# A decoder layer with sparse attention on one core: attention blocks from small to large, feature tiles and the output projection as work between them, the spatial gate per token tile

## The chip, the cores and the metric

One Trainium2 chip, of which one core runs the kernel. The metric is the device time of one execution in microseconds (us), the median of several runs. The engines of the core are TensorE (PE in the profile; PEld is its loading of weights), VectorE (DVE), ScalarE (ACT), GpSimd (POOL) and SyncE (SP), which issues most of the DMAs. Each engine works through its instructions in one fixed order and waits by semaphores for the others.

## The reference, cut to what matters

One inference step of a one-layer hybrid decoder: 1024 prompt tokens and eight sample sequences of one token each, model width 1024, all in fp32. In this cut, `u, v, z_a` belong to a gated MLP of eight channel groups of 64, the rest to a sparse attention of eight query heads and two key heads.

```python
hn = rms_norm(x, norm_g)
u, v, z_a, q, kc, vc, ks, vs, kw, vw, g, z_b = split(hn @ w_in)
vn = layer_norm(v, ln_g, ln_b)
s = einsum('bnsgc,gts->bntgc', vn, w_s * tril) + b_s     # per chunk of 128 tokens
a_out = u * s * silu(z_a)
kcc, vcc = compress(kc, w_ck, pe_ck), compress(vc, w_cv, pe_cv)   # 32 tokens -> 1, stride 16
for each block of 128 queries:
    o = gate0 * attention(q, kcc, vcc) + gate1 * attention(q, selected ks, vs) \
        + gate2 * attention(q, kw, vw within 512 tokens)
y = x + concat(a_out, o * silu(z_b)) @ w_out
return rms_norm(y, final_g), new keys and values, ...
```

The sample sequences do the same with their cached keys and values, 256 tokens each.

## The kernel before

**Numbers.** Every large operand is split into a high and a low part of a shorter format (`xh`, `xl` of the input, `whi`, `wlo` of a weight tile: ACT casts the high part, line 139, VectorE subtracts for the low one, line 140). A product is three matmuls: high by high, high by low, low by high. `mm` (line 44) is the one line in which nearly all matmuls are issued.

**Stages.** The input is loaded and split, and the features (columns of `w_in`) are made in tiles of 128 columns over all 1032 tokens, in three thirds of 344 tokens: a tile is 8 (k) x 3 products x 3 thirds = 72 matmuls named `pf`. First eight tiles for `u` and `z_a` (`uz`), then four of `q`, which go to HBM as `qd`. Then come nine token tiles of `v` (`ptv`) with their layer norm, and the spatial gate for all chunks at once (lines 384 to 421: matmuls `pg`, bias, transposes `pgt`, multiply, store to `ad`). Then the keys and values per token tile (`pta`, `ptb`), and `compress(kv)` for keys (0) and values (1) (lines 546 to 620): the prompt's part is transposed (`pct`), the cached pages come by sixteen DMAs (`cA`, line 556), both are split into `Xh` and `Xl` (lines 565 to 568), and 32 matmuls `pc` (line 587) sum over them. Four feature tiles for `silu(z_b)` (`gate_tile`) stand between and behind these, with weights loaded in a pool of their own (`wp2`).

**Attention.** Query blocks go from 7 (the longest) to 0. Each has four units of two heads; a unit's `scores` (matmuls `S`, then masks, maxima and exponentials into `Pl`, `Pw`) runs one unit ahead of the `values` of the unit before (transposes `pt`, casts `th` and differences `tl`, matmuls `o`). The function `together` interleaves these generators with a third, the filler: in block 7 `sample_attention`, in the later ones `project(qb)` of the block before (48 matmuls `pout` and their final norm), whose matmuls have a lower priority:

```python
                    with tc.high_priority(FILL):
                        mm(ps, mix[:, 0, k, :], woh[:, k, cs_], k == 0, False)
```

The scheduler orders each engine's instructions by these priorities before the kernel runs; nothing is reordered on the chip. `load_wo` (lines 652 to 656) brings the output weights, after block 7, in eight steps: DMA into one of two `wost` buffers, ACT cast to `woh`, GpSimd subtraction to `wol`. A buffer that is reused waits for its last reader; `woh` and `wol` take the memory of `xh` and `xl`. At the end come `project_s` (the samples' projection, matmuls `pouts`) and the last block's `project`.

## Time and profile before

| | |
|---|---|
| median of three runs | 731.09 us (730.53 to 731.97) |
| profiled execution | 731.21 us, its span 729.1 us |
| TensorE busy | 694.0 us (95%) |
| VectorE, ACT, GpSimd busy | 491.7, 374.6, 261.5 us |
| mean granted TensorE clock | 0.985 of full |
| chain that ended last | TensorE 48%, VectorE 19%, issue 4% |

The span is from the first to the last instruction of one profiled execution; the time holds 2.1 us more around it. Busy times are sums of the instructions' own durations, overlaps taken once. Matmuls overlap each other, so a TensorE that counts as busy need not be at its full pace. The granted clock of TensorE is 1 for 2.4 GHz and 0.5 for 1.2 GHz; between them, a mean.

### The profile page before, as it was taken

What the parts mean: (1) busy time and instruction counts of PE and PEld (TensorE: products, weight loads), DVE (VectorE), ACT (ScalarE), POOL (GpSimd) and SP (SyncE); (2) the same over time, 40 slices, a digit from 0 to 9 for tenths busy, and PEclk for the clock granted to TensorE, in tenths of its full rate; (3) what the DMA queues carried; (4) which work ended last, traced back from release to release, by engine and by line L of the source; (5) the groups of instructions that cost most, each with busy time, mean ns of one, the idle gap of its engine ahead of it and who ended that gap; (6) DMA issues with size and microseconds to landing.
All of it is one profiled execution on the core that took longest, in us unless ns stands there. A gap on an engine that the chain in (4) does not pass through costs nothing.

```text
span 729.1 us, 12274 instructions
## 1 busy us (share of the span) xinstructions
PE 694.0 (95%) x4166; PEld 622.7 (85%) x4166; DVE 491.7 (67%) x1454; ACT 374.6 (51%) x896; POOL 261.5 (36%) x234
## 2 busy tenths in 40 slices
PE   8999999999899999999899999899989999899894
PEld 7999999988699999978758888799979879688683
DVE  6655336555895622636387869977897887989945
ACT  7432212222334532433177668775775867866722
POOL 1202114213531000220173649865474473723402
PEclk9999999999989999999999999999999999999997
DMA  8441124560135401612790203511302213311111
GB/s 329 166 131 45 44 47 145 129 143 34 32 116 159 124 21 54 185 42 76 190 332 6 59 17 114 146 58 59 73 16 77 55 69 77 102 45 73 52 39 59
DMA packets 48662, 68.19 MB, mean 94 GB/s; under 512 B 4512, under 2 KB 35088, under 8 KB 47288
## 3 DMA queue, kind: packets, MB, share of 16 engines
q1 hardware_dynamic: 48152, 64.99, 29.9%
q0 software_dynamic: 160, 2.15, 0.9%
q8 instruction: 33, 0.54, 0.3%
q10 hardware_dynamic: 288, 0.27, 0.1%
q14 instruction: 29, 0.24, 0.1%
HBM read 52.11 MB, written 17.37 MB: 95 GB/s over the span
## 4 chain that ended last, share of the span: by engine, by line
PE 48%; DVE 19%; issue 4%; DMA 2%; ACT 2%; POOL 2%; SPq 1%; DVEq 0%; ACTq 0%; POOLq 0%
PE pout L44 10%; PE o L44 6%; PE pf L44 6%; PE pt L774 6%; PE S L44 6%; PE ptb L44 5%; DVE tl L778 3%; PE pc L44 3%; PE pta L44 3%; DVE Pw L729 2%; DVE Pl L693 2%; DVE r L745 2%; PE po L44 1%; PE pouts L44 1%; DMA tril<-in_tril 1%
## 5 line engine op out<-in xcount | busy, mean ns | idle before, releaser
L778 DVE TENSOR_TENSOR tl<-pt,th 128x512 fp32r<-128x512 f32 (+1 forms) x160 | 101.0, 643 | 23.0 <-ACT th L777 22.7
L777 ACT CAST th<-pt 128x512 fp32r<-128x512 f32 (+1 forms) x160 | 85.5, 551 | 46.6 <-PE pt L774 42.7
L44 PE MATMUL pout<-woh,mix 128*128 128x512 f32 (+1 forms) x272 | 88.1, 391 | 0.5 <-ACT mix L795 0.4
L751 POOL TENSOR_TENSOR Pw<-Pw,r 128x640 f32<-128x640 f32 (+3 forms) x112 | 74.9, 688 | 35.7 <-PE pt L774 9.2
L44 PE MATMUL pf<-xl,whi 128*128 128x344 f32 x384 | 86.8, 321 | 0.0
L44 PE MATMUL pf<-xh,whi 128*128 128x344 f32 x384 | 84.8, 322 | 1.0 <-ACT xh L194 1.0
L44 PE MATMUL pf<-xh,wlo 128*128 128x344 f32 x384 | 85.6, 319 | 0.0
L44 PE MATMUL o<-th,v 128*128 128x256 f32 x264 | 74.6, 302 | 1.6 <-DVE r L744 1.0
L751 POOL TENSOR_TENSOR Pl<-Pl,r 128x1024 f32<-128x1024 f32 (+5 forms) x36 | 49.0, 1362 | 73.2 <-DVE r L745 53.3
L44 PE MATMUL o<-tl,v 128*128 128x256 f32 x264 | 70.1, 292 | 4.4 <-DVE tl L778 4.1
L44 PEld LDWEIGHTS pf<-xh,whi 128*128 128x128 f32 x384 | 64.8, 188 | 2.0 <-ACT xh L194 1.9
L44 PEld LDWEIGHTS pf<-xl,whi 128*128 128x128 f32 x384 | 65.6, 189 | 0.7 <-DVE xl L195 0.3
L44 PEld LDWEIGHTS pf<-xh,wlo 128*128 128x128 f32 x384 | 65.0, 188 | 0.2
L139 ACT CAST whi<-wst 128x512 fp32r<-128x512 f32 (+2 forms) x50 | 28.5, 590 | 69.1 <-PE pf L44 58.0
L44 PE MATMUL S<-kwS,q 128*128 128x384 f32 (+2 forms) x224 | 54.9, 341 | 5.5 <-DVE nmx L693 4.9
L44 PEld LDWEIGHTS o<-tl,v 128*128 128x128 f32 x264 | 49.8, 188 | 10.8 <-DVE tl L778 8.6
L44 PEld LDWEIGHTS pout<-woh,mix 128*128 128x128 f32 x272 | 50.4, 191 | 9.2 <-ACT mix L795 0.6
L697 ACT ACTIVATE Pl<-Pl,nmx 128x1024 f32<-128x1024 f32 (+7 forms) x64 | 49.9, 779 | 15.0 <-DVE nmx L693 14.8
L44 PE MATMUL S<-ksS,q 128*128 128x512 f32 (+5 forms) x192 | 53.3, 366 | 2.0 <-DVE r_y L96 0.8
L140 DVE TENSOR_TENSOR wlo<-wst,whi 128x512 fp32r<-128x512 f32 (+2 forms) x50 | 36.4, 744 | 26.8 <-ACT whi L139 26.6
L44 PEld LDWEIGHTS o<-th,v 128*128 128x128 f32 x264 | 49.7, 188 | 4.8 <-ACT th L777 1.7
L44 PE MATMUL pout<-wol,mix 128*128 128x512 f32 (+1 forms) x136 | 52.7, 387 | 0.0
(322 smaller groups left out, 1631.9 us busy)
## 6 DMA issues: line engine op xcount, KB each, us to landing
q<-qd SPq DMA_DIRECT2D x16, 512.0 KB, 7.2
wst<-in_wF SPq DMA_DIRECT2D x26, 256.0 KB, 3.2
raw<-in_xw SPq DMA_DIRECT2D x7, 708.0 KB, 5.1
wost<-in_w_out SPq DMA_DIRECT2D x8, 512.0 KB, 9.7
xt<-in_x_prompt SPq DMA_DIRECT2D x8, 512.0 KB, 3.4
out<-xt SPq DMA_DIRECT2D x7, 512.0 KB, 2.6
wst<-in_wTv SPq DMA_DIRECT2D x8, 256.0 KB, 3.7
qd<-qh SPq DMA_DIRECT2D x8, 256.0 KB, 3.4
```

What stands on the lines that cost most here:

```text
L44: pe.matmul(out, lhsT, rhs, start=start, stop=stop, skip_group_check=True)
L139: s.copy(hi[:, :n], st[:, :n])
L140: v.tensor_tensor(lo[:, :n], st[:, :n], f32(hi[:, :n]), op=ALU.subtract)
L693: v.tensor_tensor_reduce(Pl[:, sl], S[:, 0:half], m, -0.125, nmx[:, 0:1] if c else BIG, ALU.add, ALU.min, nmx[:, 0:1])
L697: s.activation(Pl[:, 0:L], Pl[:, 0:L], AF.Exp, bias=nmx[:, 0:1], scale=-1.0, accum_out=sums[:, 1:2])
L729: v.tensor_tensor_reduce(dst, sin, m, -0.125, nmx[:, 1:2] if c else BIG, ALU.add, ALU.min, nmx[:, 1:2])
L745: v.tensor_tensor(r, r, gates[:, qb, 3 * hd:3 * hd + 3], op=ALU.mult)
L751: g.tensor_tensor(t_[:, a:b], t_[:, a:b], r[:, j:j + 1].to_broadcast((P, b - a)), op=ALU.mult)
L774: pe.transpose(pt[:, ci * 256 + e * P:ci * 256 + (e + 1) * P], src[e][:, col:col + P], ident)
L777: s.copy(th[:, :n], pt[:, :n])
L778: v.tensor_tensor(tl[:, :n], pt[:, :n], f32(th[:, :n]), op=ALU.subtract)
```

## The change

Five things. Blocks go from 0 to 7. Nine of the sixteen feature tiles (of the MLP's eight all but the first three, and the four of `silu(z_b)`) become a generator, `feature_tiles`, that works third by third in one PSUM bank at the low priority, with the low halves of its weights subtracted by GpSimd; 18 of its 108 steps stand behind `compress(0)`, six behind `compress(1)`, twelve behind `sample_attention`, which is no filler any more, and 72 in the blocks 0 to 3. Behind block 3 come the output weights, and `output()`, the projection of the samples and of blocks 0 to 6, is the filler of blocks 4 to 7; the attention outputs of blocks 0 to 3 wait for it in HBM (`od`), and `open_mix` joins them with the two gates. The spatial gate is computed per token tile inside the `v` loop, with `v` as the stationary operand, which gives it channel-major without transposes. And `Xh` and `Xl` of `compress` have their eight sub-positions outermost, so that `pc` reads them contiguously; `cA` is loaded for each `kv` apart.

```diff
+EARLY = 4
...
-        zd = dram.tile([8, P, 4, P], F32, name="zd")
-        ad = dram.tile([8, P, 4, P], F32, name="ad")
+        zd = dram.tile([4, P, T], F32, name="zd")
+        ad = dram.tile([4, P, T], F32, name="ad")
+        sd = dram.tile([4, P, T], F32, name="sd")
+        ud = dram.tile([P, TT], F32, name="ud")
+        od = dram.tile([8, P, 4, P], F32, name="od")
...
+        def load_w(src, cols, kk=1, e=v):
...
-            v.tensor_tensor(lo[:, :n], st[:, :n], f32(hi[:, :n]), op=ALU.subtract)
+            e.tensor_tensor(lo[:, :n], st[:, :n], f32(hi[:, :n]), op=ALU.subtract)
...
-        for i in range(1, 4):
-            if i > 1:
-                uF = f_tiles(0)
-                wts = f_weights(2 * i)
-                for k in range(KT):
-                    f_k(wts, uF, k)
...
+        def gate(i, vh, vl):
+
+            sp = vp.tile([P, 4, P], F32, tag="sp", bufs=2, name="sp")
+            for half in range(2):
+                ps = (ps_o, ps_p)[half]("pg")
+                for x in range(2):
+                    gp = 2 * half + x
+                    cs = slice(gp * P, gp * P + P)
+                    out = ps[:, x * 256:x * 256 + 256]
+                    mm(out, vh[:, cs], wsh[:, 2 * gp:2 * gp + 2, :], True, False)
+                    mm(out, vl[:, cs], wsh[:, 2 * gp:2 * gp + 2, :], False, False)
+                    mm(out, vh[:, cs], wsl[:, 2 * gp:2 * gp + 2, :], False, True)
+                for r in range(2):
+                    rows = slice(64 * r, 64 * r + 64)
+                    v.tensor_tensor(sp[rows, 2 * half:2 * half + 2, :],
+                                    ps[rows].rearrange("p (a r t) -> p r a t", a=2, r=2)[:, r],
+                                    bsb[rows, 2 * half:2 * half + 2, :], op=ALU.add)
+            cols = slice(i * P, (i + 1) * P)
+            g.tensor_tensor(uz[:, 0, cols], uz[:, 0, cols], sp[:, 0, :], op=ALU.mult)
+            sy.dma_start(sd[1:4, :, cols].rearrange("g p c -> p g c"), sp[:, 1:4, :])
...
+        def feature_tiles(bank):
+
+            todo = [("z", 1, 3), ("u", 2, 4), ("z", 2, 5), ("u", 3, 6), ("z", 3, 7)] + \
+                   [("b", t, 12 + t) for t in range(4)]
+            nxt = f_weights(todo[0][2], g)
+            u = ftp.tile([P, TT], F32, tag="u", name="u")
+            sy.dma_start(u, ud)
...
+                for j in range(3):
+                    ps = bank()("pf")[:, 0:CH]
+                    for k in range(KT):
+                        hi, lo = wts[k // 4]
+                        c = (k % 4) * P
+                        with tc.high_priority(FILL):
+                            f_mm(hi[:, c:c + P], lo[:, c:c + P], [ps], k, (j,))
+                        if k % 2:
+                            yield
...
+                    sy.dma_start((ad if what == "z" else zd)[i, :, cols], z[:, 0:n_p])
...
-                for j in range(16):
-                    sy.dma_start(cA[:, :, j, :], io["cA"][bass.ds(prow[j], 1)].rearrange("o k p c -> p (o k) c"))
                 sy.dma_start(Cc, io["Cc"])
                 sy.dma_start(Sc, io["Sc"])
+            cA = cx2.tile([P, 16, P], F32, tag="cA", name="cA")
+            for j in range(16):
+                sy.dma_start(cA[:, j, :], io["cA"][bass.ds(prow[j], 1), kv].rearrange("o p c -> p (o c)"))
...
-            Xh = cx2.tile([P, NSLOT, 8], F32R, tag="Xh", name="Xh")
-            Xl = cx2.tile([P, NSLOT, 8], F32R, tag="Xl", name="Xl")
+            Xh = cx2.tile([P, 8, NSLOT], F32R, tag="Xh", name="Xh")
+            Xl = cx2.tile([P, 8, NSLOT], F32R, tag="Xl", name="Xl")
...
-                split(lambda x: x[:, h * SLOT + 64:h * SLOT + 192, :].rearrange("p (a m) j -> p a (m j)", m=8),
-                      cA[:, kv, :, h * 64:h * 64 + 64], g)
+                split(lambda x: x[:, :, h * SLOT + 64:h * SLOT + 192].rearrange("p j (a m) -> p a j m", m=8),
+                      cA[:, :, h * 64:h * 64 + 64].rearrange("p a (m j) -> p a j m", j=8), g)
...
-                        mm(pc[:, 0:386], w2[:, half * 8 + j, :], x[:, half:half + 386, j], n == 0, n == 31)
+                        mm(pc[:, 0:386], w2[:, half * 8 + j, :], x[:, j, half:half + 386], n == 0, n == 31)
...
         compress(0)
-        gate_tile(0)
+        for _ in _take(features, 18):
+            pass
         compress(1)
...
+        for _ in _take(features, 6):
+            pass
+        sample_attention()
+        for _ in _take(features, 12):
+            pass
+        sm_ctx.close()
...
+        def open_mix(B):
+
+            rows = slice(B["qb"] * P, (B["qb"] + 1) * P)
+            mix = B["mix"] = mixp.tile([P, 2, KT, P], F32R, tag="mix", name="mix")
+            sy.dma_start(f32(mix[:, 1, 0:4, :]), ad[:, :, rows].rearrange("t p c -> p t c"))
+            szb = mixp.tile([P, 4, P], F32, tag="szb", bufs=1, name="szb")
+            sy.dma_start(szb, zd[:, :, rows].rearrange("t p c -> p t c"))
+            if B["qb"] < EARLY:
+                oT = mixp.tile([P, 4, P], F32, tag="oTe", bufs=1, name="oTe")
+                sy.dma_start(oT, od[B["qb"]])
+            else:
+                oT = B["oT"]
+            s.copy(mix[:, 0, 0:4, :], f32(mix[:, 1, 0:4, :]))
+            g.tensor_tensor(mix[:, 1, 0:4, :], f32(mix[:, 1, 0:4, :]), f32(mix[:, 0, 0:4, :]), op=ALU.subtract)
+            e = v if B["qb"] == 7 else g
+            e.tensor_tensor(oT, oT, szb, op=ALU.mult)
             s.copy(mix[:, 0, 4:8, :], oT)
...
-                    mm(ps, mixS[:, k, :], woh[:, k, cs_], k == 0, False)
-                    mm(ps, mixS[:, k, :], wol[:, k, cs_], False, k == KT - 1)
+                    with tc.high_priority(FILL):
+                        mm(ps, mixS[:, k, :], woh[:, k, cs_], k == 0, False)
+                        mm(ps, mixS[:, k, :], wol[:, k, cs_], False, k == KT - 1)
+                    if k % 4 == 3:
+                        yield
...
+        def output():
+
+            yield from project_s()
+            open_mix(blocks[0])
+            for qb in range(7):
+                ahead = qb + 1 < 7 and qb + 1 in closed
+                if ahead:
+                    open_mix(blocks[qb + 1])
+                yield from project(blocks[qb])
+                if qb + 1 < 7 and not ahead:
+                    open_mix(blocks[qb + 1])
-        todo = [(qb, h, tp) for qb in range(7, -1, -1) for h in range(2) for tp in range(2)]
+        todo = [(qb, h, tp) for qb in range(8) for h in range(2) for tp in range(2)]
...
-        gate_tile(2)
-        gate_tile(3)
...
+            closed.add(qb)
+            if qb < EARLY:
+                sy.dma_start(od[qb], blocks[qb]["oT"])
+            if qb == EARLY - 1:
                 for _ in fill:
                     pass
...
+                ft_ctx.close()
+                mixp = top.enter_context(tc.tile_pool(name="mixp", bufs=2, side="right", reuse_waits="tile"))
+                fg = xp.tile([P, D], F32, tag="row", name="fg")
+                sy.dma_start(fg, io["final_g"].partition_broadcast(P))
+                woh = xp.tile([P, KT, D], F32R, tag="wh", name="woh")
+                wol = xp.tile([P, KT, D], F32R, tag="wl", name="wol")
+                for k in range(KT):
+                    load_wo(k)
+                fill, left = output(), 4 + 7 * 8
...
+        open_mix(blocks[7])
+        project_last(blocks[7])
```

The order of TensorE's instructions behind the last key and value matmuls (`ptb`), where `compress(0)` begins (`pk` and `pct` are transposes), before:

```order
L44 MATMUL ptb<-wlo,xsS 128x408
L522 MATMUL pk<-ident,kvs 128x8 x2
L573 MATMUL pct<-ident,kvc 128x128 x4
L44 MATMUL pf<-xh,whi 128x344 x2
L44 MATMUL pf<-xl,whi 128x344 x2
L44 MATMUL pf<-xh,wlo 128x344 x2
```

and of the change:

```order
L45 MATMUL ptb<-wlo,xsS 128x408
L507 MATMUL pk<-ident,kvs 128x8 x2
L615 MATMUL pct<-ident,kvc 128x128 x12
L45 MATMUL pc<-Xh,w_2630 128x386
L45 MATMUL pf<-xh,whi 128x344
L45 MATMUL pf<-xl,whi 128x344
...
L45 MATMUL pc<-Xl,w_2630 128x386
```

Before, `pf` matmuls of a feature tile stand between the transposes and the `pc`; of the change all twelve transposes, one `pc` and six `pf` come ahead of the `pc` that read `Xl`.

TensorE's order where the output weights are first used, before (in block 6):

```order
L44 MATMUL pout<-woh,mix 128x512
L44 MATMUL S<-kwS,q_4340 128x384 x2
L44 MATMUL o<-th,v_2095 128x256
...
L774 MATMUL pt<-ident,Pl 128x128 x2
L774 MATMUL pt<-ident,Pw 128x128 x2
...
L44 MATMUL pout<-wol,mix 128x512
L44 MATMUL pout<-woh,mix 128x512 x2
```

and of the change, behind the last feature tile:

```order
L45 MATMUL pf<-xh,whi 128x344
L45 MATMUL pf<-xl,whi 128x344
L45 MATMUL pf<-xh,wlo 128x344
L45 MATMUL pouts<-woh,mixS 128x512
L45 MATMUL pouts<-wol,mixS 128x512
```

The first uses of the weights were single `pout` among the work of attention; of the change they are 16 `pouts` in a row, behind the last `pf`.

GpSimd's order at `load_wo`, before:

```order
L656 TENSOR_TENSOR wol<-wost,woh 128x1024 x2
L794 TENSOR_TENSOR oT<-oT,szb 128x512
L751 TENSOR_TENSOR Pl<-Pl,r 128x896
L751 TENSOR_TENSOR Pw<-Pw,r 128x640
L751 TENSOR_TENSOR Pw<-Pw,r 128x64
L656 TENSOR_TENSOR wol<-wost,woh 128x1024
L751 TENSOR_TENSOR Pw<-Pw,r 128x640
L751 TENSOR_TENSOR Pw<-Pw,r 128x64
L796 TENSOR_TENSOR mix<-oT,mix 128x512
L656 TENSOR_TENSOR wol<-wost,woh 128x1024
```

and of the change (`oTe` is the attention output read back):

```order
L1000 MEMSET mixS 128x1024
L783 TENSOR_TENSOR wol<-wost,woh 128x1024 x2
L926 TENSOR_TENSOR mix<-mix 128x512
L928 TENSOR_TENSOR oTe<-oTe,szb 128x512
L926 TENSOR_TENSOR mix<-mix 128x512
L783 TENSOR_TENSOR wol<-wost,woh 128x1024
L930 TENSOR_TENSOR mix<-oTe,mix 128x512
L783 TENSOR_TENSOR wol<-wost,woh 128x1024
L928 TENSOR_TENSOR oTe<-oTe,szb 128x512
```

The subtractions `wol` stood among those of attention (`Pl`, `Pw`); of the change all eight stand together, with the memset of `mixS`, the splits of `mix` and the products of `oTe` between them.

## Rows read from the trace of the kernel before

**Rows 1.** The page, busy us of each engine (share of the span) and its instructions.
```profile
PE 694.0 (95%) x4166; PEld 622.7 (85%) x4166; DVE 491.7 (67%) x1454; ACT 374.6 (51%) x896; POOL 261.5 (36%) x234
```
**Rows 2.** Windows (bounds in us, length, busy us and instructions of each engine, granted clock, DMA), full ones.
```profile
80.00:100.00 20.00, 20.00 (x128) 20.00 (x128) 5.85 (x12) 2.97 (x6) 2.93 (x1) 1.00 0.19 53
480.00:500.00 20.00, 20.00 (x120) 17.87 (x119) 12.92 (x44) 11.16 (x24) 11.43 (x11) 1.00 0.08 27
```
**Rows 3.** Timeline of TensorE: start, us, what, how many; four transposes in a row.
```profile
506.89 0.60 PE L774 MATMUL pt<-ident,Pw 128*128 128x128 f32 x4
```
**Rows 4.** Instructions of TensorE in 380 to 700, grouped: count | busy us, mean ns | idle before.
```profile
L44 PE MATMUL o<-th,v 128*128 128x256 f32 x261 | 73.7, 302 | 1.6 <-DVE r L744 1.0 <-DVE oT L787 0.6
...
L44 PE MATMUL pout<-woh,mix 128*128 128x512 f32 x211 | 73.2, 407 | 0.5 <-ACT mix L795 0.4
...
L774 PE MATMUL pt<-ident,Pw 128*128 128x128 f32 x304 | 49.5, 274 | 1.5 <-DVE tl L778 1.5
L44 PE MATMUL S<-kwS,q 128*128 128x384 f32 (+1 forms) x206 | 49.2, 335 | 3.2 <-DVE nmx L693 2.6 <-DVE nmx L735 0.4
```
**Rows 5.** What VectorE waited for before line 396 (us, times).
```profile
  DMA tril<-in_tril: 7.5, 1
```
**Rows 6.** Windows, with waits.
```profile
180.00:220.00 40.00, 36.92 (x185) 32.02 (x184) 34.45 (x96) 14.09 (x29) 18.09 (x14) 0.91 0.23 67
...
198.00:206.00 8.00, 6.79 (x22) 5.92 (x22) 7.93 (x17) 6.12 (x13) 1.87 (x2) 0.57 0.49 133
...
360.00:366.00 6.00, 3.66 (x11) 2.47 (x9) 5.93 (x19) 2.14 (x5) 1.49 (x1) 0.74 0.82 228
...
620.00:640.00 20.00, 16.80 (x109) 13.86 (x109) 18.83 (x71) 17.77 (x58) 14.46 (x19) 1.00 0.43 119
```
**Rows 7.** Timeline of TensorE, its last matmul.
```profile
718.76 0.28 PE L44 MATMUL pout<-woh,mix 128*128 128x256 f32 x1
```
**Rows 8.** Timeline of TensorE, two of the pc matmuls, in a row.
```profile
312.01 0.50 PE L44 MATMUL pc<-Xl,w 128*128 128x386 f32 x1
312.34 0.50 PE L44 MATMUL pc<-Xh,w 128*128 128x386 f32 x1
```
**Rows 9.** Timelines of SP, ACT and GpSimd around compress(0), and the page's DMA issues.
```profile
290.42 4.30 SPq L556 DMA_DIRECT2D cA<-in_cA  x7
...
300.39 0.54 SPq L557 DMA_DIRECT2D Cc<-in_Cc  x1
...
303.11 2.00 ACT L567 CAST Xh<-cA 128x1024 fp32r<-128x1024 f32 x2 [3.33 <-DMA Sc<-in_Sc]
...
304.23 5.23 POOL L568 TENSOR_TENSOR Xl<-cA,Xh 128x1024 fp32r<-128x1024 f32 x2 [83.30 <-DMA qsd<-kvs]
...
cA<-in_cA SPq DMA_DIRECT2D x16, 128.0 KB, 3.0
```
**Rows 10.** Window beside it.
```profile
300.00:310.00 10.00, 10.00 (x66) 9.87 (x65) 6.18 (x8) 3.15 (x6) 5.23 (x2) 1.00 0.41 120
```
**Rows 11.** Timelines and groups around load_wo, and the page's DMA issues.
```profile
432.70 4.77 POOL L656 TENSOR_TENSOR wol<-wost,woh 128x1024 fp32r<-128x1024 f32 x2
...
L796 POOL TENSOR_TENSOR mix<-oT,mix 128x512 fp32r<-128x512 f32 x7 | 9.1, 1298 | 1.5 <-ACT mix L795 1.5
...
437.41 0.48 PE L44 MATMUL pout<-wol,mix 128*128 128x512 f32 x1
...
xt<-in_x_prompt SPq DMA_DIRECT2D x8, 512.0 KB, 3.4
```
**Rows 12.** VectorE's weight splits of 512 columns, grouped.
```profile
L140 DVE TENSOR_TENSOR wlo<-wst,whi 128x512 fp32r<-128x512 f32 x34 | 24.7, 736 | 25.1 <-ACT whi L139 25.0
```
**Rows 13.** Timelines of VectorE and GpSimd at the end.
```profile
721.95 0.16 DVE L96 SCALAR_TENSOR_TENSOR r_y<-r_a,r_y 128x1 f32<-128x1 f32 x1
...
722.45 2.06 DVE L96 SCALAR_TENSOR_TENSOR r<-r_a,r_y 128x1 f32<-128x1 f32 x1
...
722.16 2.33 POOL L907 TENSOR_TENSOR xts<-xts,fg 8x1024 f32<-8x1024 f32 x1 [1.33 <-ACT xts L906]
```

More of the change, by code (lines that the diff above doesn't have):

```diff
@@ L126, in trunk @@
         RS = xp.tile([P, TT], F32, tag="row", name="RS")
-        xsS = xsp.tile([P, KT, P], F32R, name="xsS")
-        g.memset(f32(xsS), 0.0)
-        def load_w(src, cols, kk=1):
+        RSv = [RS[:, j * CH:(j + 1) * CH] for j in range(3)]
+        W = {}
+        def load_w(src, cols, kk=1, e=v):
             n = kk * cols
-            wp = wpool[0]
-            st = wp.tile([P, 512], F32, tag="wst", bufs=wpool[1], name="wst")
+            wp = W["pool"]
+            st = wp.tile([P, 512], F32, tag="wst", bufs=W["raw"], name="wst")
             with tc.issue_after(x_in.ins):
@@ L536, in trunk, with bank @@
+        N_FT = 9 * 12
+        at_bank = [0]
+        banks = [ps_s, ps_b]
+        def bank():
+            at_bank[0] += 1
+            return banks[at_bank[0] % len(banks)]
+        features = feature_tiles(bank)
         cx = ExitStack()
@@ L915, in project @@
             sy.dma_start(xt, io["x_prompt"][0, rows, :])
[L916 to L922 removed]
+            for a in (0, 512):
+                cs_ = slice(a, a + 512)
+                ps = ps_p("pout")
                 for k in range(KT):
@@ L1019, in trunk @@
             if i + 1 < len(todo):
-                others.append((first_half(i + 1, nxt), n_scores(todo[i + 1][0])))
-            if i % 4 == 0:
-                open_rest(blocks[qb])
-            part = left // (4 - i % 4)
+                q, h1, tp1 = todo[i + 1]
+                others.append((scores(blocks[q], h1, tp1, nxt), n_scores(q)))
+            part = -(-left * units[0] // sum(units))
             left -= part
@@ L1027, in trunk @@
             chunks = nxt
-            if i % 4 == 3:
+            if i % 4 != 3:
+                continue
+            closed.add(qb)
+            if qb < EARLY:
+                sy.dma_start(od[qb], blocks[qb]["oT"])
+            if qb == EARLY - 1:
                 for _ in fill:
                     pass
-                close_block(blocks[qb])
-                if qb == 7:
-                    woh = xp.tile([P, KT, D], F32R, tag="wh", name="woh")
-                    wol = xp.tile([P, KT, D], F32R, tag="wl", name="wol")
-                    for k in range(KT):
-                        load_wo(k)
-                fill, left = project(qb, blocks[qb]["mix"]), 8
-        last_s = project_s()
-        for gen, n in ((last_s, 1), (fill, 5), (last_s, 1), (fill, 8)):
-            for _ in _take(gen, n):
-                pass
+                ft_ctx.close()
[4 more added lines that the diff above has]
+                wol = xp.tile([P, KT, D], F32R, tag="wl", name="wol")
+                for k in range(KT):
+                    load_wo(k)
+                fill, left = output(), 4 + 7 * 8
+        for _ in fill:
+            pass
+        open_mix(blocks[7])
+        project_last(blocks[7])
 def _take(gen, n):
```

471 lines of the change are left out of this document (217 added, 254 removed).

## The prediction

> **What bounds the kernel now.** I read the page's busy times first: TensorE is busy 694.0 of 729.1 us, VectorE 491.7, GpSimd 261.5 [rows 1]. So the time is TensorE's work at its dense pace, plus every stretch in which it is not fed. The windows give the pace: in 80 to 100 us, where it only does feature matmuls of 344 columns, 128 of them fill 20.00 us, 0.156 us each, which is 2.2 columns per ns [rows 2]. That is far below the 321 ns that one lasts, because they overlap; all prices of matmuls below are start to start. A 512-column one is then 0.233, a 256-column one 0.116, one of 386 columns 0.175. A transpose of 128 columns is slower: four last 0.60 us and one 0.274, so the pace is (0.60 - 0.274)/3 = 0.108 [rows 3, 4].
>
> Then I looked for the stretches that are not dense. There are four. (a) 180 to 220 us, the spatial gate: VectorE waited 7.5 us for the triangle's DMA, and the granted clock in 198 to 206 is 0.57, so that most of them passed at the lower level, 1.2 GHz [rows 5, 6]. TensorE's 3.1 us idle in 180 to 220 and what the low clock costs (6.79 us busy times 0.43, 2.9) make some 6 us, and a little behind 220. (b) 360 to 380, the first scores: 3.66 of 6 us busy in 360 to 366 at clock 0.74 [rows 6]; some 8 us with the thin stretch behind it. (c) Attention, 380 to 700. Grouped by operation, and each row taken with its twin for the other half of the operand (262 beside 261 of o, 106 of pout, 276 of pt, 172 of S), TensorE does 523 o at 0.116, 317 pout at 0.233, 580 pt at 0.108 and 378 S, by their lengths of some 350 columns, at 0.16 [rows 4]: 60.7 + 73.9 + 62.6 + 60.5 = 258 us, and by the same paces some 22 for the smaller groups. 280 of 320: it loses 40. The windows say where: 480 to 500, with output projection to fill, is full, 620 to 640 is busy 16.80 with VectorE at 18.83 [rows 2, 6]. (d) The end: the last matmul is over at 719.04 [rows 7], 10 us before the span is.
>
> **The change part by part, against the 729.1 us span.** The profiled execution is 731.21 us, 2.1 above its span, and 0.1 above the median of 731.09.
>
> TensorE's own work. pc: 64 matmuls, now one per 0.33 us with the moving operand at a stride of eight elements [rows 8]; made contiguous they should run at 0.175: -9.8 us. No row shows this tile contiguous, so the bounds are 0 and -9.8; every contiguous operand here runs at 2.2 columns per ns, so I take -9.8. The gate per token tile takes 96 matmuls of 256 columns for 48, and four transposes for 32: 48 x 0.116 - 28 x 0.108 = +2.6. Together **-7**.
>
> The stride goes to the splits instead: ACT and GpSimd now read cA at a stride of eight where they read runs of 64. [rows 9] show them unstrided, 1.00 us each on ACT (two in 2.00) and 2.62 on GpSimd; I price them unchanged, and keep as the other end the factor that pc's stride costs, 0.33/0.175 = 1.9. The Trainium skill (SBUF — State Buffer, Specifications) says that SBUF is read in lines of 16 bytes, with a penalty unless at least two accesses hit each line. The trace agrees for pc at 0.33 us, and no run here shows it for ACT or GpSimd; by the rule it speaks against the change.
>
> The gate stage. Its weights come before the v tiles, so the 7.5 us wait goes, while VectorE gets 32 small adds instead of 8 large multiplies in a loop with the layer norms. Between 0 and -7, I take **-4**.
>
> compress(0). Before, the 16 cache loads begin to issue at 290.42 us while feature matmuls run, and the last GpSimd half of Xl ends at 309.46; TensorE is full in 300 to 310 [rows 9, 10]. After, the memory of Cc is the one that xsS held, so SP's Cc waits for the last ptb matmul, and all 16 cA loads stand behind it; the feature weights stand behind those. TensorE's row is in order: pk, twelve pct, one pc, six pf, then 31 pc that need Xl. From the last ptb: Cc and Sc 1.1, sixteen issues at 0.61 9.9 (the same count, half the bytes), landing 3.0, first Xh 1.0, two Xl 5.2: 20.2 us. The work in between is 0.1 + 1.3 + 0.2 + 0.9 = 2.5. **+18**, bounds 12 (no wait for the issues of the smaller loads beyond half of theirs) and 24 (strided splits, 0.9 x (1.0 + 5.2) = +5.6).
>
> compress(1), sample attention, first block. compress(1) has 18 feature steps (8 us) ahead of its chain and six behind: **+2**, bounds 0 and 8. Sample attention ran as filler through block 7; now it stands alone, its softmax and copies in a row, with 6 and 12 steps of features about it. I put its waits and the start of block 0 at 11 us, against the 8 of (b): **+3**, bounds -3 and +10.
>
> Attention. All blocks now have filler: features in 0 to 3, the projection in 4 to 7. If every block became like 480 to 500, the loss of 40 would fall to some 5; if the waits are the softmax chain's as in 620 to 640 it stays. GpSimd takes 18 weight halves from VectorE. I take 20 as left: **-20**, bounds 0 and -35. The Trainium skill (SBUF — State Buffer, Who interferes with whom) says that GpSimd and a VectorE operation with two SBUF operands exclude each other for a whole instruction, so VectorE would wait for those halves. The trace agrees at its end, where r, the operation that took 0.16 just before, lasts 2.06 us beside GpSimd's 2.33 [rows 13]. In rows: 18 halves of 512 columns at 1.30 us [rows 11] are 23 us, against 13 us that VectorE no longer spends (0.74 each [rows 12]), so at worst 10 us more on VectorE, inside the bounds.
>
> load_wo, after block 3. woh and wol lie in the memory of xh and xl, so the first ACT copy waits for the last feature matmul. In TensorE's order, the sixteen pouts follow that matmul at once, and every second one needs the next wol. From there: the last feature's way to zd on ACT, VectorE and SP (whose wost loads stand behind it) some 1.8, landing 3.4, ACT 1.0 as for Xh [rows 9]: 6.2 us. Then GpSimd, in order: eight wol of 2.39 (two in 4.77) and, between them, seven mix and oT operations of 1.30, 28.2 us [rows 11]. The last wol is there after 34.4 us, in which TensorE has 16 x 0.233 = 3.7 us to do. **+31**, bounds 22 (nothing between the eight) and 36 (a landing later by as much as the two wost buffers hold it up, one ACT copy and one issue). Before, the same subtractions were spread from 432.70 on between attention's own; the first pout started at 437.41, where the second wol ended (432.70 + 4.77), and other matmuls stood between the pouts [rows 11].
>
> Clock. After (a)'s gap it was 0.57 over 8 us [rows 6]; two longer gaps are new: **+4**, bounds 2 and 8. The first q tile's weights wait for the first pool: **+1**. End: project_s no longer covers block 7's gate, four operations of 512 columns in a row on ACT and VectorE (at 0.74 [rows 12], +3), nor holds up r for 2 us [rows 13]: **+1**.
>
> Sum: -7 - 4 + 18 + 2 + 3 - 20 + 31 + 4 + 1 + 1 = +29. Span 758, time **760 us**.
>
> **The rivals.**
> 1. The gains outweigh (faster). Were attention to lose only 5 (-35) and both gaps be smaller, the sum of the two gaps decides: everything else is then -35 - 7 - 4 + 11 = -35, so they must stay under 35 us together, where I count 49. That needs TensorE or GpSimd to do something else in the order that I read; with gaps of 20 in all the time is 716. For it: attention's 40 us are real. Against: both gaps are chains of operations whose lengths stand in rows. Without that gain in attention the limit is 20.
> 2. Only one gap opens: compress(0) is covered, as in 300 to 310 [rows 10]: 742. Against: there are six pf in TensorE's order, not sixty.
> 3. Attention gains nothing, because VectorE sets it: 780. For it: 18.83 of 20 us busy in 620 to 640 [rows 6].
> 4. The strided splits cost 1.9 times as much: compress(0) +5.6, compress(1) about +2: 768. This is what the 16-byte rule would make of it.
> 5. The kernel comes out level, within 0.2% (about what a measurement can tell from no change): gains and gaps would have to cancel.
>
> **How the numbers follow.** Forecast with attention between -8 and -32, 0.60, range 748 to 774; rival 4 inside that 0.10; rival 3 at 774 to 785, 0.09; rival 2 at 734 to 748, 0.08; rival 1 0.10; rival 5 0.03. Faster 0.10, same 0.03, slower 0.87. The range reaches to rivals 2 and 3: 738 to 780, which leaves out rivals 1 and 5, half of 3 and the lower part of 2, some 0.19.
>
> **What the next profile would show.** A hole of 17 to 19 us in TensorE between ptb and the second pc, with SP issuing cA in it. A hole of some 31 us between the last pf and the attention of block 4, in which pouts start one per wol. pc at 0.175 start to start. Fuller windows in attention before and after, at about 9.4 of 10 us. It is wrong if pouts do not wait there, if cA lands before ptb ends, or if blocks 0 to 3 show VectorE busy through and TensorE waiting.

## The result, and the profile after

The changed kernel takes 777.17 us (median of four, 776.26 to 779.87) beside 731.53 of the kernel before: ratio 1.0626, 95% interval 1.0589 to 1.0662. The forecast was 760, slower, with a range of 738 to 780. The profiled execution is 777.74 us with a span of 776.0, 46.9 more than before.

The page of the changed kernel: busy us of each engine, the slices of TensorE, of its clock and of VectorE, and the chain that ended last.

```profile
PE 692.6 (89%) x4186; PEld 634.4 (82%) x4186; DVE 488.3 (63%) x1463; ACT 376.3 (48%) x881; POOL 302.5 (39%) x279
...
PE   8989996989997588979999999823999999999994
...
DVE  6638692896614073125999888501576688788863
...
PEclk9999998999998598989999999955899999999997
...
PE 71%; DMA 8%; DVE 7%; POOL 4%; SPq 3%; issue 3%; ACT 2%; POOLq 0%; DVEq 0%; ACTq 0%
```

TensorE is as busy as before [rows 1] in a span 47 us longer. Apart from the last slice, it is lowest in 14, at 5, and in 27 and 28, at 2 and 3; there the clock is at 5 and VectorE at 0 in 14 and 27. Slice 7, at 6, is the gate stage. The chain is TensorE for 71% against 48% before: outside the holes the kernel is bound by its own matmuls.

Windows by stage of the changed kernel (columns as in [rows 2]): gate, `compress(0)`, `compress(1)`, sample attention and first block, blocks 0 to 3, `load_wo`, blocks 4 to 7.

```profile
60.00:135.00 75.00, 68.90 (x364) 62.05 (x364) 49.15 (x70) 19.95 (x34) 26.88 (x13) 0.95 0.47 132
...
245.00:280.00 35.00, 19.75 (x101) 18.44 (x100) 13.32 (x31) 14.52 (x25) 10.64 (x6) 0.71 0.56 164
280.00:310.00 30.00, 24.02 (x132) 23.48 (x131) 14.93 (x25) 11.32 (x21) 18.15 (x15) 0.89 0.23 73
310.00:362.00 52.00, 45.06 (x256) 36.66 (x255) 14.07 (x62) 9.80 (x41) 9.76 (x11) 0.90 0.48 144
362.00:502.00 140.00, 139.71 (x1006) 136.82 (x1005) 121.22 (x464) 102.33 (x308) 67.55 (x89) 1.00 0.25 74
502.00:552.00 50.00, 21.48 (x61) 12.73 (x59) 5.73 (x16) 14.99 (x21) 28.12 (x16) 0.59 0.50 157
552.00:755.00 203.00, 201.98 (x1276) 183.44 (x1276) 159.37 (x503) 133.97 (x293) 108.44 (x93) 1.00 0.20 62
```

Attention is dense on both sides of the hole, at full clock: 139.71 of 140 and 201.98 of 203 us, where before 620 to 640 was 16.80 of 20 [rows 6]. To say what each stage loses, I priced every matmul of a stretch by the prediction's start-to-start paces and took the sum from its length; the rest is waiting, thin work and low clock. The losses are estimates, good to some 4 us, since the smaller matmuls have no pace of their own in the rows; the first row follows from the prices.

| lost beyond dense work, us | before | after | difference | forecast |
|---|---|---|---|---|
| dense work itself | 654.0 | 646.9 | -7 | -7 |
| start, with a wait for the input's norm | 3.3 | 7.3 | +4 | +1 |
| gate stage | 9.5 | 14.3 | +5 | -4 |
| `compress(0)`, 245 to 280 | under 1 | 19.6 | +19 | +18 |
| `compress(1)`, 280 to 310 | under 1 | 9.3 | +9 | +2 |
| sample attention, first block, 310 to 362 | 9.5 | 15.9 | +6 | +3 |
| attention | 40 | 9.9 | -30 | -20 |
| `load_wo`, 502 to 552, its low clock with it | 0 | 39.4 | +39 | +31, clock +4 |
| end | 10.5 | 12.8 | +2 | +1 |

The differences add up to +47, where the spans differ by 46.9.

What TensorE waited for in the changed kernel (us in total, times, longest):

```profile
PE pouts L45 <- POOL wol L783: 18.0, 8, 3.2
PE pouts L45 <- ACT woh L782: 9.4, 4, 7.6
PE pc L45 <- ACT Xh L609: 9.0, 1, 9.0
PE pbs L361 <- POOL bsx L358: 6.1, 1, 6.1
```

Timeline of the changed kernel around `compress(0)` (start, us, what, how many; in brackets the idle time before it and its releaser):

```profile
243.93 0.35 PE L45 MATMUL ptb<-wlo,xsS 128*128 128x408 f32 x1
...
244.31 0.65 SPq L596 DMA_DIRECT2D Cc<-in_Cc  x1
...
245.83 1.96 SPq L600 DMA_DIRECT2D cA<-in_cA  x4
...
249.00 6.01 SPq L600 DMA_DIRECT2D cA<-in_cA  x12
...
256.69 3.98 ACT L609 CAST Xh<-cA 128x1024 fp32r<-128x1024 f32 x2 [4.79 <-DMA pce<-in_pe_c]
...
258.79 5.62 POOL L610 TENSOR_TENSOR Xl<-cA,Xh 128x1024 fp32r<-128x1024 f32 x2 [70.43 <-DMA wst<-in_wF]
...
260.86 0.69 PE L45 MATMUL pc<-Xh,w 128*128 128x386 f32 x1 [9.01 <-ACT Xh L609]
...
264.47 0.69 PE L45 MATMUL pc<-Xl,w 128*128 128x386 f32 x1 [0.99 <-POOL Xl L610]
```

The last `ptb` frees the memory, only then does SP issue `Cc` and the sixteen `cA`, and the `pc` that read `Xl` start 20.2 us after `Cc`: the forecast chain, with its length.

Around `load_wo`:

```profile
502.10 0.32 PE L45 MATMUL pf<-xh,wlo 128*128 128x344 f32 x1
...
504.50 3.45 SPq L781 DMA_DIRECT2D wost<-in_w_out  x2
...
508.92 1.04 ACT L782 CAST woh<-wost 128x1024 fp32r<-128x1024 f32 x1
...
510.01 0.79 PE L45 MATMUL pouts<-woh,mixS 128*128 128x512 f32 x1 [7.60 <-ACT woh L782]
510.04 4.78 POOL L783 TENSOR_TENSOR wol<-wost,woh 128x1024 fp32r<-128x1024 f32 x2 [1.30 <-ACT woh L782]
...
525.89 1.26 POOL L928 TENSOR_TENSOR oTe<-oTe,szb 128x512 f32<-128x512 f32 x1 [1.57 <-DMA oTe<-od]
...
535.56 4.65 POOL L783 TENSOR_TENSOR wol<-wost,woh 128x1024 fp32r<-128x1024 f32 x2
...
540.27 0.79 PE L45 MATMUL pouts<-wol,mixS 128*128 128x512 f32 x1 [1.09 <-POOL wol L783]
```

For 38 us TensorE does sixteen `pouts`. The wait is the forecast one, some 1.7 us later at its head (508.92 for the first cast) and 2 us longer in GpSimd (30.2 for 28.2), which waited 1.57 and 1.36 us for `oTe` to be read back.

### The profile page after: what moved, and what is told of

Same layout as the page of the kernel before. It is cut to its first block, busy times and chain, and to the rows that moved or that the text cites. A ratio compares the mean times of both kernels' runs of the same rounds, so it can differ in the third digit from the quotient of the medians.

```text
span 776.0 us, 12627 instructions
## 1 busy us (share of the span) xinstructions
PE 692.6 (89%) x4186; PEld 634.4 (82%) x4186; DVE 488.3 (63%) x1463; ACT 376.3 (48%) x881; POOL 302.5 (39%) x279
## 4 chain that ended last, share of the span: by engine, by line
PE 71%; DMA 8%; DVE 7%; POOL 4%; SPq 3%; issue 3%; ACT 2%; POOLq 0%; DVEq 0%; ACTq 0%
PE pf L45 16%; PE pout L45 11%; PE o L45 9%; PE S L45 9%; PE pt L896 8%; PE ptb L45 5%; PE ptv L45 3%; PE pta L45 2%; DMA wst<-in_wF 2%; SPq L600 1%; PE po L45 1%; DVE wlo L141 1%; PE pc L45 1%; PE pA L45 1%; PE pg L45 1%
## 5 line engine op out<-in xcount | busy, mean ns | idle before, releaser
L45 PE MATMUL pf<-xh,whi 128*128 128x344 f32 x384 | 110.6, 329 | 2.0 <-ACT xh L197 1.1
L45 PE MATMUL pf<-xl,whi 128*128 128x344 f32 x384 | 111.2, 325 | 0.0
L45 PE MATMUL pf<-xh,wlo 128*128 128x344 f32 x384 | 110.1, 323 | 0.7 <-DVE wlo L141 0.7
L900 DVE TENSOR_TENSOR tl<-pt,th 128x512 fp32r<-128x512 f32 (+1 forms) x160 | 101.3, 643 | 14.0 <-ACT th L899 12.8
L873 POOL TENSOR_TENSOR Pl<-Pl,r 128x384 f32<-128x384 f32 (+5 forms) x36 | 49.1, 1364 | 92.5 <-DVE r L867 37.4
L45 PEld LDWEIGHTS pf<-xh,whi 128*128 128x128 f32 x384 | 70.2, 191 | 5.8 <-ACT xh L197 2.2
L45 PEld LDWEIGHTS pf<-xl,whi 128*128 128x128 f32 x384 | 70.6, 191 | 1.6 <-issue 1.0
L819 ACT ACTIVATE Pl<-Pl,nmx 128x128 f32<-128x128 f32 (+7 forms) x64 | 49.7, 777 | 33.7 <-DVE nmx L815 26.4
L859 ACT ACTIVATE Pw<-Pw,nmx 128x640 f32<-128x640 f32 (+4 forms) x64 | 44.6, 696 | 25.5 <-DVE nmx L851 23.3
L45 PE MATMUL S<-ksS,q 128*128 128x384 f32 (+5 forms) x192 | 53.1, 362 | 2.3 <-DMA q<-qd 1.9
L896 PE MATMUL pt<-ident,Pw 128*128 128x128 f32 x304 | 49.4, 274 | 0.0
```

The lines of the kernel that those rows point to most:

```text
L45: pe.matmul(out, lhsT, rhs, start=start, stop=stop, skip_group_check=True)
L819: s.activation(Pl[:, 0:L], Pl[:, 0:L], AF.Exp, bias=nmx[:, 0:1], scale=-1.0, accum_out=sums[:, 1:2])
L859: s.activation(Pw[:, 0:nw], Pw[:, 0:nw], AF.Exp, bias=nmx[:, 1:2], scale=-1.0, accum_out=sums[:, 2:3])
L873: g.tensor_tensor(t_[:, a:b], t_[:, a:b], r[:, j:j + 1].to_broadcast((P, b - a)), op=ALU.mult)
L896: pe.transpose(pt[:, ci * 256 + e * P:ci * 256 + (e + 1) * P], src[e][:, col:col + P], ident)
L900: v.tensor_tensor(tl[:, :n], pt[:, :n], f32(th[:, :n]), op=ALU.subtract)
```

## The experiments

The theory: two places where memory is handed over late (`Cc`'s and `woh`'s) open holes as long as the reload, 58 us together, which the denser attention pays back by half. The rivals: that the loss is spread, by GpSimd against VectorE or by the clock, so that closing a hole gains little; and, for each cure, that its work is missing elsewhere. "Gain" below is the difference of the ratio to the 1.0626 of the changed kernel, times 731 us; edits are of the changed kernel where nothing else is said.

**Output projection later.** Block 4 takes no filler.

```diff
             part = -(-left * units[0] // sum(units))
+            if qb == EARLY:
+                part = 0
```

> The changed kernel, with block 4's four units left without filler, so that the first pouts stand behind block 4 in TensorE's order; load_wo stays where it is. Theory A (the 36 us hole behind the last pf is an order's: the sixteen pouts stand ahead of block 4, whose own work needs no output weights): the hole closes, block 4 runs in it at some 8 us of loss, the later blocks hold the projection as well: 777 - 36 - 4 (low clock) + 8, some 745 us. Rival B (block 4 has to wait for something else of that moment, its queries or the memory that the feature tiles leave): the hole stays at over 20 us under other names, 765 us or more.

769.39 us, ratio 1.0516 (1.0488 to 1.0544), a gain of 8. Filler of a low priority is not held back by that: the scheduler put the last feature steps into block 4 and the `pouts` early again, with some 9 us of attention between, and they waited 15.5 us for `wol`. The load now shared the queues of ACT, GpSimd and SP with attention's work and ended at 566.

**Features ahead of compress(0).** 18 steps of features stand ahead of it as well as behind it.

```diff
+        for _ in _take(features, 18):
+            pass
         compress(0)
...
-        left = N_FT - 36
+        left = N_FT - 54
```

> The changed kernel with 18 feature steps (108 pf, 16.8 us at 0.156) ahead of compress(0) as well as the 18 behind it, taken from blocks 0 to 3, so that their weight loads stand ahead of most cA loads in SP's queue. Theory A (TensorE lacks work there because the weights stand behind cA): the 17 us hole behind ptb is filled but for some 4 us until the first weights are there, the low clock there goes too, blocks 0 to 3 lose a little more: some 762 us. Rival B (the chain through SP, ACT and GpSimd only gets longer by what the weights add to these queues): the hole moves to just before the pc, and the time stays within 4 us of 777.

761.28 us, 1.0396 (1.0362 to 1.0429): a gain of 17, but not all of it in this hole. In 240 to 280 TensorE is busy 31.95 us where it was 24.75 (6.61 and 18.14). Priced as in the table, the stretch from the last `ptb` to the last `pc` of `compress(0)` loses 12.7 us where it lost 19.6: the 16.8 us of matmuls closed 7 of it. What is left is a wait of 5.7 us for the first of those features' own weights, one of 2.4 for `Xh`, and 10 us at half clock.

```profile
PE pouts L45 <- POOL wol L785: 11.6, 4, 6.1
...
PE pf L45 <- ACT whi L140: 5.7, 1, 5.7
...
PE pouts L45 <- ACT woh L784: 3.2, 2, 1.8
```

Another 5 us come at `load_wo`: the `pouts` wait 14.8 us in all where they waited 27.4, since the features end earlier and some 10 us of attention now stand between the last `pf` and the first `pouts`. Up to that last `pf` the blocks, with 54 steps of filler for 72, lose no more of their time than in the changed kernel.

**pc's layout alone, in the kernel before,** with the splits that write it.

```diff
-            Xh = cx2.tile([P, NSLOT, 8], F32R, tag="Xh", name="Xh")
-            Xl = cx2.tile([P, NSLOT, 8], F32R, tag="Xl", name="Xl")
+            Xh = cx2.tile([P, 8, NSLOT], F32R, tag="Xh", name="Xh")
+            Xl = cx2.tile([P, 8, NSLOT], F32R, tag="Xl", name="Xl")
...
-                        mm(pc[:, 0:386], w2[:, half * 8 + j, :], x[:, half:half + 386, j], n == 0, n == 31)
+                        mm(pc[:, 0:386], w2[:, half * 8 + j, :], x[:, j, half:half + 386], n == 0, n == 31)
```

> The kernel before with only the layout of Xh and Xl changed, as in the changed kernel. Theory A (pc is on TensorE's path and the rest is covered by the gate tiles): 64 x (0.327 - 0.175) = 9.7 us less, 721.5 us; the strided splits (Xh 1.99 for 1.00 us each on ACT, Xl 2.8 to 3.1 for 2.6 on GpSimd in the changed kernel) cost nothing there. Rival B (the splits come late here too, by 2 x 1.0 + 2 x 0.3 per compress): 724 to 727 us.

729.89 us, 0.9988 (0.9965 to 1.0011): level, though `pc` did get faster. The first `S` starts at 351.25 where before it was 359.10, so 7.9 us of the 9.8 are there. They are lost by 409, where the lead is 0.4. VectorE, GpSimd and TensorE of this kernel:

```profile
394.23 1.66 DVE L849 TENSOR_SCALAR sa_wl<-sa_wl 64x3 f32<-64x3 f32 x1
...
399.42 1.89 POOL L751 TENSOR_TENSOR Pl<-Pl,r 128x1024 f32<-128x1024 f32 x1 [2.09 <-DVE r L745]
...
399.61 3.37 DVE L855 TENSOR_SCALAR sa_wl<-sa_wl 64x128 f32<-64x128 f32 x3
...
401.27 1.56 POOL L751 TENSOR_TENSOR Pw<-Pw,r 128x640 f32<-128x640 f32 x2
...
402.73 0.64 PE L860 MATMUL pT<-ident,sa_wl 64*128 64x64 f32 x5 [2.44 <-DVE sa_wl L855]
```

Three scalings of the sample softmax (line 855), 0.88 us together in the kernel before, fell onto GpSimd's `Pl` and `Pw` and took 3.37 us; the transposes behind them waited 2.44, and the clock was at half from 403.8 to 407.2. An operation of three columns (line 849), 0.16 us in the kernel before, had fallen onto an earlier `Pl` and taken 1.66, and an `S` waited 1.41 us behind it.

**The same with the scalings on ACT, and the scalings on ACT alone,** both of them edits of the kernel before; this diff is the whole of the second.

```diff
-                v.tensor_scalar(Sl[:, a:b], Sl[:, a:b], sm[:, j:j + 1], None, op0=ALU.mult)
+                s.activation(Sl[:, a:b], Sl[:, a:b], AF.Copy, scale=sm[:, j:j + 1])
```

> The kernel before with the layout of Xh and Xl changed, as in the earlier trial that came out level, and the last scaling of the sample's probabilities (three operations of line 855, which lasted 3.37 us on VectorE beside a subtraction of GpSimd's where the trial lost its lead) on ACT. Theory A (the 8 us that contiguous pc gains were given back in that collision and in the half clock behind it): the lead stays to the end, 722 to 725 us. Rival B (attention's chain on VectorE takes it back anyway, in one place or another): 728 us or more.

> The kernel before with only line 855's three operations on ACT, its layout of Xh and Xl unchanged: the control of the trial with both edits, which took 9 us off. Theory A (pc's layout is the gain, and the move to ACT only keeps it): within 2 us of the kernel before, 729 to 733 us. Rival B (the move itself, or the schedule that comes with it, is the gain): 722 to 726 us.

With both: 722.06 us (six runs, 719.63 to 724.46), 0.9879 (0.9858 to 0.9901), 1.2% under the kernel before and clear of the interval. With the scalings alone: 725.29, 0.9925 (0.9905 to 0.9945). With both, the scalings take 1.22 us on ACT while GpSimd works on the same `Pw`:

```profile
399.98 1.50 POOL L751 TENSOR_TENSOR Pw<-Pw,r 128x640 f32<-128x640 f32 x2
...
400.54 1.22 ACT L855 ACTIVATE sa_wl<-sa_wl 64x128 f32<-64x128 f32 x3
```

The lead of the 73rd `S` is then 5.0 us where it was 0.4, so that collision had eaten 4.6 of the 7.5 us. Most of the other 2.9 were lost ahead of it in both kernels, with the wait behind line 849 (1.66 us here too), which no edit moved. But the scalings alone lead by only 0.2 us at that place and by 5.5 in the last `pout`; that comes in from 640 on, in another interleaving of the last blocks, and in the same way in the kernel with the layout (its lead goes from 5.8 to 11.4). Why the scheduler's new order is better there stays open. The spans of the two profiled executions, 717.7 and 723.6, differ by 5.9; the medians by 3.2. So the layout is worth some 3 of its 9.8 us here.

**The gate's bias early.** `bs` comes with the constants, and ACT instead of GpSimd widens it.

```diff
-        g.tensor_copy(bsx, bs.unsqueeze(2).to_broadcast((P, 8, 64)))
+        s.copy(bsx, bs.unsqueeze(2).to_broadcast((P, 8, 64)))
...
```

> The changed kernel with the gate's bias loaded at the start and widened by ACT, not by GpSimd behind the product of the gate's weights and the triangle. Theory A (the wait of the four pbs transposes, 6.1 us, is GpSimd's queue: the widening stands behind a product that waits for the triangle's late DMA): the wait goes and the half clock behind it (121.6 to 128.4 us) with it: 6.1 + 3.4, some 768 us. Rival B (the stage is set by the layer norms on VectorE and GpSimd anyway): TensorE waits for vh or the sums soon after, 774 us or more.

774.69 us, 1.0593 (1.056 to 1.0626): a gain of 2, within the intervals. In the changed kernel the transposes of the bias waited for GpSimd, whose copy `bsx` stood behind the triangle's product, which waited for a DMA:

```profile
116.43 0.44 SPq L350 DMA_DIRECT2D tril<-in_tril  x1
...
122.14 2.34 POOL L355 TENSOR_TENSOR ws<-ws,tril 128x1024 f32<-128x1024 f32 x1 [15.52 <-DMA tril<-in_tril]
124.42 0.61 POOL L358 COPY bsx<-bs 128x512 f32<-128x512 f32 x1
...
125.09 1.12 PE L361 MATMUL pbs<-ident,bsx 128*128 128x128 f32 x4 [6.10 <-POOL bsx L358]
```

With the bias early that wait is gone, and the next one behind the same triangle stands in its place:

```profile
121.22 2.41 POOL L355 TENSOR_TENSOR ws<-ws,tril 128x1024 f32<-128x1024 f32 x1 [15.62 <-DMA tril<-in_tril]
...
128.32 2.49 POOL L402 TENSOR_TENSOR vt<-vt,lnb 128x512 f32<-128x512 f32 x2
...
130.29 0.79 PE L45 MATMUL pg<-wsh,vh 128*128 128x256 f32 x2 [6.75 <-ACT vh L406]
```

**wol on VectorE.** Is `load_wo`'s hole GpSimd's throughput, or the chain through two `wost` buffers?

```diff
-            g.tensor_tensor(wol[:, k, :], st, f32(woh[:, k, :]), op=ALU.subtract)
+            v.tensor_tensor(wol[:, k, :], st, f32(woh[:, k, :]), op=ALU.subtract)
```

> The changed kernel with the eight wol subtractions on VectorE, which did nothing in that hole, instead of GpSimd. Theory A (the hole is GpSimd's queue: eight wol at 2.35 and seven products and splits of 1.27, 28 of its 38 us): the sixteen pouts are done when landing, ACT and VectorE's eight of some 1.45 us are, the hole shrinks by 15 us or more, to some 760 us. Rival B (the two wost buffers: each next load waits for a subtraction, then 0.4 us of issue, 3.0 of landing, 1.0 of ACT, so that a pair takes 6 us also with a fast subtraction): 8 to 9 us less, some 768 us.

769.30 us, 1.0521 (1.0487 to 1.0555): a gain of 8, not the 18 by which the sum of one engine would shrink (8 x 1.11, and 8.9 for GpSimd's seven other operations, no longer in between).

```profile
507.86 1.23 DVE L783 TENSOR_TENSOR wol<-wost,woh 128x1024 fp32r<-128x1024 f32 x1 [0.72 <-ACT woh L782]
...
509.12 2.93 SPq L781 DMA_DIRECT2D wost<-in_w_out  x2
...
515.65 3.04 DVE L783 TENSOR_TENSOR wol<-wost,woh 128x1024 fp32r<-128x1024 f32 x2 [3.98 <-ACT woh L782]
```

VectorE needs 1.23 us where GpSimd needs 2.34, and later idles 3.98 between two of them: a new `wost` is issued only when a subtraction has freed its buffer, and pairs come some 7 us apart (issues at 502.16, 509.12, 517.59, 524.09).

**All features ahead of attention,** 30, 30, 18 and 30 steps in the four places; `load_wo` at attention's start, the projection as filler from block 2.

```diff
+        for _ in _take(features, 30):
+            pass
         compress(0)
-        for _ in _take(features, 18):
+        for _ in _take(features, 30):
             pass
...
-        for _ in _take(features, 6):
+        for _ in _take(features, 18):
             pass
         sample_attention()
-        for _ in _take(features, 12):
+        for _ in features:
             pass
...
```

> The changed kernel with all 108 feature steps ahead of attention (30 ahead of compress(0), 30 behind it, 18 behind compress(1), 30 behind sample attention), load_wo at the start of attention and the output projection as filler of blocks 2 to 7. If the two chains of compress and load_wo's are what the change lost, and any work closes them: the 17 us hole at compress(0), 6 at compress(1), some 6 in sample attention and 36 at load_wo go, with the low clock behind them, 65 to 70 us in all; attention, with 85 us of filler where it had 152, gives back some 20 of the 30 that it gained: 727 to 735 us. Rival (attention's gain came of the filler in every block and is lost whole, and load_wo still holds up GpSimd's and SP's queues in blocks 0 and 1): 745 us or more.

770.96 us, 1.0528 (1.0499 to 1.0557): a gain of 7. The waits of `pouts` are gone and `compress(0)`'s hole is as small as in the experiment with 18 steps; 400 to 470, with blocks 0 and 1, which have no filler, and the load beside them, loses some 35 us.

**Small blocks bare.** The 72 steps of blocks 0 to 3 stand ahead of block 0; nothing else is moved.

```diff
+        for _ in features:
+            pass
+        left = 0
...
```

> The changed kernel with all 72 feature steps of blocks 0 to 3 ahead of block 0, so that these blocks run without filler; the output weights stay behind block 3. Theory A (filler in every block is what attention gained by): blocks 0 to 3, whose 101 us of their own lose 5 now, lose some 18 to 25; the hole at load_wo shrinks, because the memory is free early, to under 10 us: some 765 us. Rival B (the order from small to large does it, since the first block starts with short chains): blocks 0 to 3 lose under 8 us more, some 745 us.

765.33 us, 1.0457 (1.0439 to 1.0474): a gain of 12. The hole at `load_wo` is down to 2.4 us of waits, since the weights arrive while blocks 0 to 3 run. But those now lose some 46 us, where the changed kernel lost 5.2. The two cancel (39 and 41), and the gain is made elsewhere, most of it ahead of block 0: some 9 us in sample attention, where the moved steps now stand among its matmuls and TensorE is busy throughout at full clock (45.06 of 52 us at 0.90 in the changed kernel). The first row below shows that stretch; the second shows the bare blocks, which are VectorE's and ACT's:

```profile
310.00:362.00 52.00, 52.00 (x318) 44.15 (x319) 12.60 (x29) 8.48 (x23) 14.73 (x14) 1.00 0.53 161
...
410.00:470.00 60.00, 44.59 (x238) 36.20 (x238) 50.43 (x203) 46.03 (x146) 35.77 (x38) 0.86 0.54 157
```

How much of the 46 is the missing filler, and how much the load's casts and subtractions on ACT and GpSimd in the same stretch, was not separated.

**Output held back.** Blocks 4 and 5 take no filler, `pouts` are tied behind a matmul of block 5, and the attention outputs of 4 and 5 go through HBM as well.

```diff
-                    with tc.high_priority(FILL):
+                    with tc.high_priority(FILL), tc.issue_after(blocks[5][1, 0].ins):
                         mm(ps, mixS[:, k, :], woh[:, k, cs_], k == 0, False)
...
+            if qb in (4, 5):
+                part = 0
...
```

> The changed kernel with blocks 4 and 5 left without filler and the first pouts tied in TensorE's order behind block 5's third unit, so that 34 us of attention's own matmuls (at the dense paces) stand between the last pf and the first pouts, where the earlier trial left 9. Theory A (the hole is an order's, and goes once enough work without output weights stands ahead of the pouts): the waits of pouts for wol and woh (27 us in the changed kernel) fall under 5, the bare blocks lose 8 to 15, some 750 us. Rival B (SP's, ACT's and GpSimd's queues take so much longer over the loads beside attention that pouts still wait): over 10 us of those waits, 760 us or more.

760.69 us, 1.0398 (1.0381 to 1.0416): a gain of 17. No `pouts` waits for a weight, and the eight subtractions are spread in the background, from 521 to 578. The bare stretch beside it loses 18 us in 520 to 560:

```profile
520.00:560.00 40.00, 31.61 (x175) 26.27 (x174) 33.41 (x97) 30.22 (x66) 37.60 (x30) 0.86 0.50 148
```

**Three cures together:** the 18 steps ahead of `compress(0)`, the bias early, and `pouts` tied behind block 4, which is bare (the diffs above, with `blocks[4]`).

> The changed kernel with three of the edits together: 18 feature steps ahead of compress(0) and 18 behind it, the gate's bias early, and the pouts tied behind block 4's third unit with block 4 left without filler (36 us of attention's own matmuls between the last pf and the first pouts). If the three act apart: 777 - 16 - 2.5, and of load_wo's hole (39 with the half clock) some 25 less: some 733 us, level with the kernel before. If the bare block 4 gives most of it back: 745 us or more.

747.89 us, 1.0222 (1.0203 to 1.0242): a gain of 30, still slower than before. Some 14 us of it come between the last `pf` and the last `pouts` and 8 at `compress(0)`; the bias gives nothing that shows. 470 to 530, with the load in it, loses some 23 us.

## Why the prediction was right in its direction and short in its size

**TensorE's own work.** Right in the one pace that was assumed: `pc` now follows at some 0.177 us, for 0.175, at the upper clock. The -7 of the table is priced by it and so no test of its own. Nearly half of the `pc` ran at the lower clock, 0.32 apart, which the table has under the two `compress`. In the kernel before, the layout alone moved nothing, since VectorE's collisions took the gain back.

**compress(0).** Right in mechanism and size, 19 for 18: 9.2 us of issues, 1.7 to ACT's first cast, two casts of 1.99 and two subtractions of 2.81 that overlap them, 20.2 us in all as forecast. That the length agrees to a tenth is luck: the landing took 1.7 for 3.0 and the issues 9.2 for 9.9, while the casts ahead of the first subtraction took 2.1 for 1.0, the subtractions 5.6 for 5.2 and `Cc` and `Sc` 1.5 for 1.1.

**The strided splits (rival 4).** Half right. ACT's cast is 1.99 us where it was 1.00, as the factor 1.9 would have it. GpSimd's `Xl` is 2.81 here, 3.10 in `compress(1)` and 3.33 with the layout in the kernel before, against 2.62: 7 to 27% more, not 90. In the chain that is about 1.4 us, not 5.6. The Trainium skill (SBUF — State Buffer, Specifications) has one rule, lines of 16 bytes, for both; ACT agrees with it, GpSimd's measured time does not show it in full.

**compress(1).** Mis-sized, 9 for 2, by two errors. The text prices 18 feature steps at 8 us; a step is six matmuls, so they are 108 x 0.156 = 16.8. That should have made the cover better, and yet a hole opened, because the splits of `pct` on ACT and VectorE, which I had not counted, ended last:

```profile
280.90 6.20 POOL L610 TENSOR_TENSOR Xl<-cA,Xh 128x1024 fp32r<-128x1024 f32 x2 [7.49 <-ACT Xh L609]
...
284.05 3.61 DVE L593 TENSOR_TENSOR w<-wst,w 128x512 fp32r<-128x512 f32 x1 [0.22 <-ACT w L592]
...
293.17 0.66 PE L45 MATMUL pc<-Xh,w 128*128 128x386 f32 x1 [5.99 <-DVE Xl L610]
```

VectorE's split of `w`, 0.69 us elsewhere, lasted 3.61 beside GpSimd's `Xl`, and four of the `pct` differences stood behind it; TensorE's gap is 6.0 us, and then the clock was 0.5 until 299. The exclusion that the prediction weighed for attention bit here. That the one long operation made the gap was read from the trace, not tried by itself; it is 2.9 us longer than elsewhere, half of the gap.

**The gate stage.** Wrong in sign, +5 for -4. The failed step is "its weights come before the v tiles, so the 7.5 us wait goes": it went from VectorE to GpSimd, whose queue has the layer norm's products in it too. The triangle's DMA is still late, and the experiment with the bias showed the next matmul taking the wait over.

**load_wo.** Right in place and mechanism; 39 for 31 and the 4 of the clock. The head was 1.7 us longer, the read-back of `oTe` added 2.9, and the clock stayed at half until 548.3. GpSimd's sum set it, but it is not alone: with the subtraction halved in length the two buffers set it, and the gain was 8.

**Attention.** Under-estimated, -30 for -20. The choice "I take 20 as left" was too careful: with filler every block runs like 480 to 500 of [rows 2], near the far end of the bounds, -35. The experiment with bare small blocks shows the other side, 46 us lost where filler left 5, though with the load beside them. GpSimd's weight halves held nothing up that shows.

**Start, sample attention, end.** Each a little short, +12 for +5 together; the start's part is a wait for the input's norm, which differs between the profiled kernels (2.5 us here, none in some of the experiments).

**Clock.** Mis-sized. TensorE's matmuls followed each other at the lower level for some 4 us behind `compress(0)`'s hole, 6 behind `compress(1)`'s and 6 behind `load_wo`'s; at half pace that is some 8 us, an estimate, for the 4 forecast, and the table has it in those rows. The mean clock fell from 0.985 to 0.939.

**The other rivals.** Rival 1 needed the two holes under 35 us; they were 58. Rival 2, one gap, and rival 3, no gain in attention, are out by the table. That the two holes and the attention make up the change is the table's, whose differences add up; the experiments bear it out in part, since none of them closed one hole and left the rest alone. With the 18 steps `compress(0)` gave back 7 of 19, as the cover's own weights came late; with the output held back `load_wo` gave back 17 of 39; with bare small blocks it gave back nothing net, since attention lost as much. All three cures gave 30 of 46, 22 of them in the two holes. Whether a version of this order beats the kernel before was not found: the best of it is 2.2% slower.

## What to carry to other kernels

Memory that one pool hands to the next makes a hole as long as the reload's whole chain (issue, landing, cast, subtraction, once per pair of buffers) unless TensorE has that much work in its order between the last reader of the old and the first reader of the new; read that order, count the cover in us of matmuls, and see when the cover's own inputs arrive: 16.8 us of features gave back 7 here, not least because their weights came late. Filler that is spent on a hole is missing elsewhere, but not evenly: 18 of the 72 steps went from the small blocks without a net loss, all 72 cost as much as the hole. Before a gain is put down to the place that an experiment was meant for, price the other stages too. A shorter operation gains only if the next stage isn't bound elsewhere, and when times shift, look for which VectorE operations now fall beside GpSimd's long ones.
